# Byte offsets of the split weights in the gate and up tiles 2 and 3 of a two-layer decoder kernel

## Chip, cores and metric

The kernel runs on one core of one Trainium2 chip. The metric is the time of one execution on the device, in microseconds (us), lower is better. The engines are named as the profile names them: PE is the matmul engine (PEld are its weight loads), DVE the vector engine, ACT the scalar engine, POOL and SP the two others. SP issues the loads of the weights.

## What is computed

The reference is a decoder trunk of two layers on 256 tokens of width 1024, in float32. Each layer has a mixer (attention and Mamba heads in layer 0, a gated delta rule in layer 1), then a gated MLP with a short convolution, then a gated per-layer embedding. The change is in the MLP:

```python
def conv_ffn(h, w_gate, w_up, conv_w, conv_b, w_down):
    gte = causal_dwconv(h @ w_gate, conv_w) + conv_b.astype(h.dtype)
    return (jax.nn.silu(gte) * (h @ w_up)) @ w_down

for i in range(DEPTH):                      # DEPTH = 2
    ...
    h = rmsnorm(x, norm_ffn[i])
    x = x + conv_ffn(h, ffn_w_gate[i], ffn_w_up[i], ffn_conv_w[i], ffn_conv_b[i], ffn_w_down[i])
    x = x + per_layer_embedding(x, p[i], norm_ple[i], ple_w_proj[i], ple_w_gate[i])
```

`w_gate` and `w_up` are 1024 x 2816, `w_down` is 2816 x 1024.

## The kernel before

Activations lie transposed: 128 channels on the partitions, 256 tokens along a row. Every product of a weight matrix is made of blocks of 128 x 128 weights, and every block is used in three matmuls, because weights and activations are each split into a high part and a low part: high weights by high activations (line 187), high weights by low activations (line 188), low weights by high activations (line 189). Each of these matmuls streams 256 columns, and the engine loads its 128 x 128 weights for each of them anew. `mm3` (lines 179 to 189) writes these triples for the blocks of one accumulation.

`piece` (lines 140 to 167) brings weights in. For up to 1024 columns (`BLK`, eight blocks) it takes a buffer `raw`, lets SP issue the load from the weight stream, lets ACT write the high part `whi` (line 162), and lets DVE or POOL write the low part `wlo` (line 163). `whi` and `wlo` have four buffers each, and every buffer begins at a multiple of 256 bytes in its partition. The parameter `lead` shifts the weights within the buffer, in float32 columns of 4 bytes. The split operations are put into the order with a raised priority (`AHEAD`), so that they run ahead of the matmuls that need them.

The activations that the matmuls stream (`xx`, `yy`, `xp` and others) come from `moving` (lines 110 to 113): they begin 48 columns, so 192 bytes, behind a multiple of 256, and since each is 1024 bytes long, all of them lie 192 bytes behind such a multiple.

`ffn` (line 275 on) is the MLP of one layer. It runs over 22 tiles `f` of 128 channels. Each tile has 24 matmuls for the gate (into `pg`) and 24 for up (into `pu`), eight blocks of three each. DVE and ACT then make scaling, convolution, SiLU and product of the tile (lines 295 to 309) while PE is at the next tiles. Then follow eight tiles of the down projection (`pd`, 66 matmuls each), the projection of the embedding (`pp`, 48 matmuls in all), a norm (`nps`, `rep`) and its gate (`pgt`, 192 matmuls).

All tiles but one take their weights as two pieces of 1024 columns with `lead` 0: the gate's, then up's. Tile `f == KICK`, which is tile 2, is split by blocks: its first seven blocks come as two pieces of 896 columns with `lead` 48, so 192 bytes behind a multiple of 256, and the eighth block of both as one piece of 256 columns with `lead` 0.

```python
if f == KICK:
    for k0, nk, lead in ((0, 7, 48), (7, 1, 0)):
        ws = self.piece([(n, i, k0, nk, f * P, P) for _, n in both], lead=lead)
        for (ps, _), w in zip(both, ws):
            self.mm3(ps[:, :T], w, self.a[k0:k0 + nk], start=k0 == 0, stop=k0 == 7)
```

Of the kernel before, what the change touches and what calls it, by code (L numbers as in the profile page):

```python
# [8 lines left out]
F32R = mybir.dt.float32r  # L9
# [7 lines left out]
P = 128  # L17
BLK = 1024
# [3 lines left out]
KICK = 2  # L22
T = 256
D = 1024
KD = D // P
# [26 lines left out]
class Trunk:  # L52
# [84 lines left out]
        yield  # L137
        self.chain = was

    def piece(self, blocks, lo=None, lead=0):  # L140

        nc = self.nc
        groups, g, cols = [], [], 0
        for b in blocks:
            n = b[3] * b[5]
            if cols + n > BLK:
                groups.append((g, cols))
                g, cols = [], 0
            g.append(b)
            cols += n  # L150
        groups.append((g, cols))
        res = []
        for g, cols in groups:
            raw = self.rawp.tile([P, BLK], F32, tag="raw", name=self.uid("raw"))
            src = self.stream[self.off:self.off + P * cols].rearrange("(p c) -> p c", p=P)
            nc.sync.dma_start(raw[:, :cols], src)
            self.off += P * cols
            self.order.append(list(g))
            hi, lo_ = (self.splp.tile([P, BLK], F32R, tag=f"w{h}", name=self.uid(f"w{h}"), align_bytes=256)
                       [:, lead:lead + cols] for h in ("hi", "lo"))  # L160
            with self.tc.high_priority(offset=AHEAD):
                nc.scalar.activation(hi, raw[:, :cols], AF.Copy)  # L162
                self.lo_engine(lo).tensor_tensor(lo_, raw[:, :cols], hi.bitcast(F32), op=ALU.subtract)  # L163
            o = 0
            for (_, _, _, nk, _, w) in g:
                n = nk * w
                res.append((hi[:, o:o + n].rearrange("p (k f) -> p k f", f=w),
                            lo_[:, o:o + n].rearrange("p (k f) -> p k f", f=w)))
                o += n
        return res  # L170
# [105 lines left out]
    def ffn(self, i, nxt):  # L276
        nc, tc = self.nc, self.tc
        with self.psum(acc=7), tc.tile_pool(name=f"ffn{i}", bufs=3) as fp:
            ys = []
            yy = self.moving(fp, 2 * NF, "yy")  # L280
            for f in range(NF):
                pg, pu = self.acc("pg"), self.acc("pu")
                both = ((pg, "ffn_w_gate"), (pu, "ffn_w_up"))
                if f == KICK:

                    for k0, nk, lead in ((0, 7, 48), (7, 1, 0)):
                        ws = self.piece([(n, i, k0, nk, f * P, P) for _, n in both], lead=lead)
                        for (ps, _), w in zip(both, ws):
                            self.mm3(ps[:, :T], w, self.a[k0:k0 + nk], start=k0 == 0, stop=k0 == 7)
                else:  # L290
                    ws = self.piece([(n, i, 0, KD, f * P, P) for _, n in both])
                    for (ps, _), w in zip(both, ws):
                        self.mm3(ps[:, :T], w, self.a)
                g = fp.tile([P, T], F32, tag="g", name=self.uid("g"))
                nc.vector.tensor_tensor(g, pg[:, :T], self.R, op=ALU.mult)
                cw = lambda t: self.v(f"fcw{i}", f * 3 + t)
                h = fp.tile([P, T], F32, tag="h", name=self.uid("h"))
                nc.scalar.activation(h, g, AF.Identity, scale=cw(2), bias=self.v(f"fcb{i}", f))
                for s in (1, 2):
                    nc.vector.scalar_tensor_tensor(out=h[:, s:], in0=g[:, :T - s], scalar=cw(2 - s), in1=h[:, s:],  # L300
                                                   op0=ALU.mult, op1=ALU.add)
                sl = fp.tile([P, T], F32, tag="sl", name=self.uid("sl"))
                si = nc.scalar.activation(sl, h, AF.Silu)
                if i == 0 and f < len(self.zb[0]):
                    with tc.issue_after(si.ins):
                        nc.scalar.activation(self.zb[0][f], self.ident.unsqueeze(1).to_broadcast([P, 4, P]), AF.Copy)
                y = fp.tile([P, T], F32, tag="y", name=self.uid("y"))
                nc.vector.tensor_tensor(y, sl, pu[:, :T], op=ALU.mult)
                yh, yl = yy[2 * f:2 * f + 2]
                self.split(y, yh, yl)  # L310
                ys.append((yh, yl))
            self.norm_begin(f"ple{i}", fp)
            Rf = self.R
            for m in range(KD):
                pd = self.acc("pd")
                for k0, nk in ((0, 8), (8, 7), (15, 7)):
                    wd, = self.piece([("ffn_w_down", i, k0, nk, m * P, P)])
                    self.mm3(pd[:, :T], wd, ys[k0:k0 + nk], start=k0 == 0, stop=k0 == 15)
                d = fp.tile([P, T], F32, tag="pleg", name=self.uid("d"), bufs=4)
                nc.vector.tensor_tensor(d, pd[:, :T], Rf, op=ALU.mult)  # L320
                nc.vector.tensor_tensor(self.x[m], self.x[m], d, op=ALU.add)
                self.norm_tile(m)
            self.ple_proj(i, fp)
            self.norm_end()
            self.ple(i, nxt, fp)
# [831 lines left out]
```

## Time and profile before

| | us |
|---|---|
| median of three runs | 934.05 |
| lowest and highest of the three | 931.06, 934.14 |
| the profiled execution, its time | 932.68 |
| its span, first to last instruction | 930.9 |

| engine | busy, share of the span |
|---|---|
| PE | 98% |
| PE weight loads | 93% |
| DVE | 80% |
| ACT | 63% |
| POOL | 5% |

A busy PE says little of its own: a matmul's record is longer than the distance to the next one, since they are pipelined. How fast PE goes is read from the distance from one matmul's start to the next one's, called the pace here. A view by stretches counts every instruction that touches the stretch, so two or three of its matmuls began before it; the stretch divided by the count without these is the pace. The records of starts in the timeline are rounded to 10 ns, so a pace is taken over many matmuls.

### The profile page before, as it was taken

What the parts mean: (1) busy time and instruction counts of PE and PEld (TensorE: products, weight loads), DVE (VectorE), ACT (ScalarE), POOL (GpSimd) and SP (SyncE); (2) the same over time, 40 slices, a digit from 0 to 9 for tenths busy, and PEclk for the clock granted to TensorE, in tenths of its full rate; (3) what the DMA queues carried; (4) which work ended last, traced back from release to release, by engine and by line L of the source; (5) the groups of instructions that cost most, each with busy time, mean ns of one, the idle gap of its engine ahead of it and who ended that gap; (6) DMA issues with size and microseconds to landing.
All of it is one profiled execution on the core that took longest, in us unless ns stands there. A gap on an engine that the chain in (4) does not pass through costs nothing. (4 is left out here: it accounts for less than half of the span.)

```text
span 930.9 us, 19991 instructions
## 1 busy us (share of the span) xinstructions
PE 909.9 (98%) x7834; PEld 870.2 (93%) x7834; DVE 747.8 (80%) x1664; ACT 584.8 (63%) x1239; POOL 42.8 (5%) x53
## 2 busy tenths in 40 slices
PE   8999999999999999999989999999999999999998
PEld 6988778999999999989889999999999999999997
DVE  6977778978777766789989998999878877776665
ACT  6576565667555545667678778777656655554452
POOL 0000112100000001020000000000001000000100
PEclk9999999999999999999999999999999999999999
DMA  7543333456555556544413332432445655555571
GB/s 274 184 131 114 113 92 113 149 161 214 185 192 190 169 186 201 169 154 152 144 56 95 118 99 92 137 112 71 137 138 164 200 187 191 189 172 187 175 221 51
DMA packets 41278, 141.40 MB, mean 152 GB/s; under 512 B 4704, under 2 KB 6496, under 8 KB 41184
## 3 DMA queue, kind: packets, MB, share of 16 engines
q1 hardware_dynamic: 40896, 139.84, 46.9%
q8 instruction: 61, 1.00, 0.4%
q10 hardware_dynamic: 288, 0.29, 0.1%
q14 instruction: 33, 0.27, 0.1%
HBM read 139.06 MB, written 1.05 MB: 151 GB/s over the span
## 5 line engine op out<-in xcount | busy, mean ns | idle before, releaser
L162 ACT ACTIVATE whi<-raw 128x1024 fp32r<-128x1024 f32 (+3 forms) x268 | 277.7, 1037 | 189.2 <-PE pd L188 45.7
L163 DVE TENSOR_TENSOR wlo<-raw,whi 128x1024 fp32r<-128x1024 f32 (+3 forms) x268 | 320.2, 1195 | 86.5 <-ACT whi L162 83.6
L187 PE MATMUL pg<-xx,whi 128*128 128x256 f32 x352 | 99.0, 281 | 0.7 <-DVE x L707 0.3
L188 PE MATMUL pg<-xx,whi 128*128 128x256 f32 x352 | 99.0, 281 | 0.0
L187 PE MATMUL pu<-xx,whi 128*128 128x256 f32 x352 | 99.0, 281 | 0.0
L187 PE MATMUL pd<-yy,whi 128*128 128x256 f32 x352 | 98.9, 281 | 0.0
L188 PE MATMUL pd<-yy,whi 128*128 128x256 f32 x352 | 98.9, 281 | 0.0
L189 PE MATMUL pd<-yy,wlo 128*128 128x256 f32 x352 | 98.9, 281 | 0.0
L188 PE MATMUL pu<-xx,whi 128*128 128x256 f32 x352 | 98.8, 281 | 0.0
L189 PE MATMUL pu<-xx,wlo 128*128 128x256 f32 x352 | 98.8, 281 | 0.0
L189 PE MATMUL pg<-xx,wlo 128*128 128x256 f32 x352 | 98.8, 281 | 0.0
L187 PE MATMUL pgd<-xx,whi 128*128 128x256 f32 x256 | 75.7, 296 | 0.4 <-DVE z L993 0.4
L189 PE MATMUL pgd<-xx,wlo 128*128 128x256 f32 x256 | 74.7, 292 | 0.0
L188 PE MATMUL pgd<-xx,whi 128*128 128x256 f32 x256 | 74.5, 291 | 0.0
L187 PEld LDWEIGHTS pg<-xx,whi 128*128 128x128 f32 x352 | 67.4, 192 | 0.8 <-issue 0.8
L187 PEld LDWEIGHTS pd<-yy,whi 128*128 128x128 f32 x352 | 67.6, 192 | 0.0
L187 PEld LDWEIGHTS pu<-xx,whi 128*128 128x128 f32 x352 | 67.5, 192 | 0.0
L189 PEld LDWEIGHTS pg<-xx,wlo 128*128 128x128 f32 x352 | 66.1, 188 | 0.0
L189 PEld LDWEIGHTS pu<-xx,wlo 128*128 128x128 f32 x352 | 66.1, 188 | 0.0
L188 PEld LDWEIGHTS pg<-xx,whi 128*128 128x128 f32 x352 | 66.1, 188 | 0.0
L188 PEld LDWEIGHTS pu<-xx,whi 128*128 128x128 f32 x352 | 66.1, 188 | 0.0
L188 PEld LDWEIGHTS pd<-yy,whi 128*128 128x128 f32 x352 | 66.1, 188 | 0.0
(357 smaller groups left out, 2632.1 us busy)
## 6 DMA issues: line engine op xcount, KB each, us to landing
raw<-stream SPq DMA_DIRECT2D x228, 512.0 KB, 3.7
raw<-stream SPq DMA_DIRECT2D x36, 448.0 KB, 3.3
x<-xT SPq DMA_DIRECT2D x4, 256.0 KB, 4.9
out<-x SPq DMA_DIRECT2D x8, 128.0 KB, 1.8
cst<-cst SPq DMA_DIRECT2D x1, 645.0 KB, 5.9
raw<-pT SPq DMA_DIRECT2D x2, 256.0 KB, 2.6
raw<-stream SPq DMA_DIRECT2D x3, 128.0 KB, 2.1
pv<-pv ACTq DMA_DIRECT2D x1, 215.5 KB, 4.5
```

Of the source, the lines that this page charges most:

```text
L162: nc.scalar.activation(hi, raw[:, :cols], AF.Copy)
L163: self.lo_engine(lo).tensor_tensor(lo_, raw[:, :cols], hi.bitcast(F32), op=ALU.subtract)
L187: nc.tensor.matmul(out, wh, ah, start=start and k == 0, stop=False)
L188: nc.tensor.matmul(out, wh, al, start=False, stop=False)
L189: nc.tensor.matmul(out, wl, ah, start=False, stop=stop and k == n - 1)
```

## The change

The special case of tile 2 goes: it is loaded as two pieces of 1024 columns, as all others are. Buffers `whi` and `wlo` become 48 columns longer, and `lead` becomes a pair, the shift of a call's first piece and of its second. Tile 2 has (0, 16) and tile 3 has (32, 48), so the gate and up weights of these two tiles lie 0, 64, 128 and 192 bytes behind a multiple of 256. All others stay at 0.

```diff
-    def piece(self, blocks, lo=None, lead=0):
+    def piece(self, blocks, lo=None, lead=(0, 0)):
...
-        for g, cols in groups:
+        for n, (g, cols) in enumerate(groups):
...
-            hi, lo_ = (self.splp.tile([P, BLK], F32R, tag=f"w{h}", name=self.uid(f"w{h}"), align_bytes=256)
-                       [:, lead:lead + cols] for h in ("hi", "lo"))
+            at = lead[n % 2]
+            hi, lo_ = (self.splp.tile([P, BLK + 48], F32R, tag=f"w{h}", name=self.uid(f"w{h}"), align_bytes=256)
+                       [:, at:at + cols] for h in ("hi", "lo"))
...
-                if f == KICK:
-
-                    for k0, nk, lead in ((0, 7, 48), (7, 1, 0)):
-                        ws = self.piece([(n, i, k0, nk, f * P, P) for _, n in both], lead=lead)
-                        for (ps, _), w in zip(both, ws):
-                            self.mm3(ps[:, :T], w, self.a[k0:k0 + nk], start=k0 == 0, stop=k0 == 7)
-                else:
-                    ws = self.piece([(n, i, 0, KD, f * P, P) for _, n in both])
-                    for (ps, _), w in zip(both, ws):
-                        self.mm3(ps[:, :T], w, self.a)
+
+                ws = self.piece([(n, i, 0, KD, f * P, P) for _, n in both],
+                                lead={KICK: (0, 16), KICK + 1: (32, 48)}.get(f, (0, 0)))
+                for (ps, _), w in zip(both, ws):
+                    self.mm3(ps[:, :T], w, self.a)
```

On PE, at the end of tile 2 in layer 0, the order before is this. `pg_2719` and `pu_2720` are tile 2's accumulators, `whi_2729` and `wlo_2730` its up weights of 896 columns at 192 bytes, `whi_2777` and `wlo_2778` the piece with the eighth block of both at 0 bytes, and `pg_2800` is tile 3's gate.

```order
L189 MATMUL pu_2720<-xx_70,wlo_2730 128x256
L187 MATMUL pg_2719<-xx_70,whi_2777 128x256
L188 MATMUL pg_2719<-xx_70,whi_2777 128x256
L189 MATMUL pg_2719<-xx_70,wlo_2778 128x256
L187 MATMUL pu_2720<-xx_70,whi_2777 128x256
L188 MATMUL pu_2720<-xx_70,whi_2777 128x256
L189 MATMUL pu_2720<-xx_70,wlo_2778 128x256
L187 MATMUL pg_2800<-xx_70,whi_2804 128x256
```

In the changed kernel, where these lines are 188 to 190, the same place reads as follows; `pg_2794` is tile 3's gate, `whi_2729` and `wlo_2730` are tile 2's up weights at 64 bytes, `whi_2798` and `wlo_2799` tile 3's gate weights at 128 bytes.

```order
L188 MATMUL pu_2720<-xx_70,whi_2729 128x256
L189 MATMUL pu_2720<-xx_70,whi_2729 128x256
L190 MATMUL pu_2720<-xx_70,wlo_2730 128x256
L188 MATMUL pg_2794<-xx_70,whi_2798 128x256
L189 MATMUL pg_2794<-xx_70,whi_2798 128x256
L190 MATMUL pg_2794<-xx_70,wlo_2799 128x256
```

The gate's three matmuls of the eighth block moved from behind up's seventh block to the end of the gate's own; nothing else moved on PE, and there are as many matmuls as before.

On DVE, during tiles 1 and 2 of layer 0, the order before is this; `wlo` are the splits of weights, the other names belong to the tiles' elementwise work.

```order
L163 TENSOR_TENSOR wlo_2730<-raw_2727,whi_2729 128x896
L308 TENSOR_TENSOR y_2640<-sl_2637,pu_2570 128x256
L295 TENSOR_TENSOR g_2706<-pg_2644,Rrep_2555 128x256
L163 TENSOR_TENSOR wlo_2778<-raw_2775,whi_2777 128x256
L214 TENSOR_TENSOR yy_2568<-y_2640,yy_2568 128x256
L300 SCALAR_TENSOR_TENSOR h_2708<-g_2706,pv,h_2708 128x255
L300 SCALAR_TENSOR_TENSOR h_2708<-g_2706,pv,h_2708 128x254
L308 TENSOR_TENSOR y_2715<-sl_2712,pu_2645 128x256
L163 TENSOR_TENSOR wlo_2805<-raw_2802,whi_2804 128x1024
```

In the changed kernel the same place on DVE reads so.

```order
L164 TENSOR_TENSOR wlo_2730<-raw_2727,whi_2729 128x1024
L304 TENSOR_TENSOR y_2640<-sl_2637,pu_2570 128x256
L291 TENSOR_TENSOR g_2706<-pg_2644,Rrep_2555 128x256
L164 TENSOR_TENSOR wlo_2799<-raw_2796,whi_2798 128x1024
L215 TENSOR_TENSOR yy_2568<-y_2640,yy_2568 128x256
L296 SCALAR_TENSOR_TENSOR h_2708<-g_2706,pv,h_2708 128x255
L296 SCALAR_TENSOR_TENSOR h_2708<-g_2706,pv,h_2708 128x254
L164 TENSOR_TENSOR wlo_2805<-raw_2802,whi_2804 128x1024
L304 TENSOR_TENSOR y_2715<-sl_2712,pu_2645 128x256
```

The small split of 256 columns is gone, and the split of tile 3's gate weights stands in its place. ACT and SP lose one instruction per layer in the same way.

## Rows read from the trace of the kernel before

**Rows 1.** The page: span, and each engine's busy time, share and instructions.

```profile
span 930.9 us, 19991 instructions
...
PE 909.9 (98%) x7834; PEld 870.2 (93%) x7834; DVE 747.8 (80%) x1664; ACT 584.8 (63%) x1239; POOL 42.8 (5%) x53
```

**Rows 2.** Stretches: length; busy (count) of PE, PEld, DVE, ACT, POOL; clock; DMA.

```profile
172.00:190.00 18.00, 18.00 (x162) 18.00 (x161) 16.54 (x24) 13.13 (x23) 4.25 (x5) 1.00 0.56 177
198.17:203.61 5.44, 5.44 (x51) 5.44 (x49) 4.27 (x9) 4.42 (x8) 0.00 (x0) 1.00 0.65 197
203.61:208.64 5.03, 5.03 (x44) 5.03 (x43) 3.32 (x5) 3.26 (x5) 0.00 (x0) 1.00 0.42 118
209.35:319.60 110.25, 110.25 (x939) 110.25 (x938) 87.47 (x139) 65.69 (x104) 0.00 (x0) 1.00 0.59 192
385.80:388.20 2.40, 2.40 (x23) 2.40 (x23) 2.19 (x9) 0.27 (x1) 0.00 (x0) 1.00 0.48 179
389.50:408.20 18.70, 18.70 (x161) 18.70 (x161) 16.69 (x31) 12.90 (x26) 3.63 (x5) 1.00 0.46 147
715.58:721.02 5.44, 5.44 (x51) 5.44 (x49) 4.37 (x9) 4.04 (x7) 0.00 (x0) 1.00 0.68 207
721.02:726.06 5.04, 5.04 (x45) 5.04 (x43) 3.22 (x5) 2.73 (x4) 0.00 (x0) 1.00 0.48 148
726.76:834.20 107.44, 107.44 (x915) 107.44 (x914) 85.67 (x137) 62.21 (x97) 0.00 (x0) 1.00 0.59 189
834.20:902.00 67.80, 67.80 (x578) 67.80 (x577) 44.53 (x55) 35.45 (x53) 5.89 (x6) 1.00 0.61 194
```

**Rows 3.** Tile pg, 198.2 to 203.4 us (tile 1): durations min/median/max, ns.

```profile
L187 PEld LDWEIGHTS pg<-xx,whi x8: 187/188/188, 198.1 to 200.4; 128*128 128x128 f32 x8
L187 PE MATMUL pg<-xx,whi x8: 276/276/276, 198.2 to 200.5; 128*128 128x256 f32 x8
```

**Rows 4.** Tile pg, 204 to 206 us (tile 2, weights at 192 bytes).

```profile
L187 PEld LDWEIGHTS pg<-xx,whi x6: 192/192/192, 203.8 to 205.6; 128*128 128x128 f32 x6
L187 PE MATMUL pg<-xx,whi x6: 283/283/283, 204.0 to 205.8; 128*128 128x256 f32 x6
```

**Rows 5.** Tile pg, 209.4 to 319.5 us (tiles 3 to 21).

```profile
L187 PEld LDWEIGHTS pg<-xx,whi x152: 192/192/192, 209.2 to 313.5; 128*128 128x128 f32 x152
L187 PE MATMUL pg<-xx,whi x152: 281/281/281, 209.3 to 313.6; 128*128 128x256 f32 x152
L188 PEld LDWEIGHTS pg<-xx,whi x152: 187/188/188, 209.4 to 313.6; 128*128 128x128 f32 x152
```

**Rows 6.** Timeline of PE, layer 0: start, duration, into and out of tile 2.

```profile
203.49 0.28 PE L189 MATMUL pu<-xx,wlo 128*128 128x256 f32 x1
203.61 0.28 PE L187 MATMUL pg<-xx,whi 128*128 128x256 f32 x1
203.73 0.28 PE L188 MATMUL pg<-xx,whi 128*128 128x256 f32 x1
...
208.53 0.28 PE L189 MATMUL pu<-xx,wlo 128*128 128x256 f32 x1
208.64 0.28 PE L187 MATMUL pg<-xx,whi 128*128 128x256 f32 x1
208.76 0.28 PE L188 MATMUL pg<-xx,whi 128*128 128x256 f32 x1
```

**Rows 7.** Lines by shape, DVE's splits: count | busy us, mean ns | idle before, releaser.

```profile
L163 DVE TENSOR_TENSOR wlo<-raw,whi 128x1024 fp32r<-128x1024 f32 x228 | 279.3, 1226 | 57.2 <-ACT whi L162 54.3
...
L163 DVE TENSOR_TENSOR wlo<-raw,whi 128x896 fp32r<-128x896 f32 x36 | 39.4, 1093 | 29.3 <-ACT whi L162 29.3
```

**Rows 8.** Timeline of DVE in layer 0: start, length, idle time before.

```profile
199.29 1.09 DVE L163 TENSOR_TENSOR wlo<-raw,whi 128x896 fp32r<-128x896 f32 x1
...
202.01 0.43 DVE L163 TENSOR_TENSOR wlo<-raw,whi 128x256 fp32r<-128x256 f32 x1
...
205.83 1.23 DVE L163 TENSOR_TENSOR wlo<-raw,whi 128x1024 fp32r<-128x1024 f32 x1 [1.05 <-ACT whi L162]
```

## The prediction

> **What bounds the kernel now.** I read the page first: PE is busy for 909.9 of 930.9 us [rows 1]. Since a busy PE can still go at different speeds, the second view is the one by stretches, and what to see there is that inside the MLPs PE fills every stretch to the last digit (5.44 of 5.44 us, 110.25 of 110.25) at a granted clock of 1.00, the 2.4 GHz level [rows 2]. So no wait ends there, neither for weights nor for DVE or ACT, and the only thing that can move the time of an MLP is PE's pace. I get it by dividing a stretch by its matmuls, less the two or three that began earlier:
>
> - tile 1 of layer 0: 5.44 us / 48 = 113.3 ns; layer 1 the same, 5.44 / 48 [rows 2];
> - tile 2, the blocks with weights at 192 bytes: 5.03 / 42 = 119.8 ns, layer 1 5.04 / 42 = 120.0 [rows 2];
> - tile 3 and on: 110.25 / 936 = 117.8 ns; in layer 1 107.44 / 912 = 117.8, and 67.80 / 575 = 117.9 through the down projection and `pp` [rows 2].
>
> All of these are the same instructions of the same shape; only the offset of the weights differs in the second, and not even that between the first and the third. The durations say the same: 276 ns a matmul and 187 to 188 a weight load in tile 1 [rows 3], 283 and 192 in tile 2 [rows 4], 281 ns and one load of three at 192, the others at 187 to 188, from tile 3 on [rows 5]. The timeline dates the changes: the step from 113 to 120 ns comes with the first matmuls whose weights lie at 192 bytes (203.49, 203.61, 203.73), and the first matmuls with weights at 0 again (208.64, 208.76) leave the 120 at once, but for 117.8 and not for 113.3 [rows 6].
>
> So offset 0 has **two paces, and the stream remembers which**. Outside the MLP's tiles this shows too: 18.00 us / 159 = 113.2 ns in layer 0's output projection, and in one and the same loop of `pgt` 2.40 / 21 = 114 ns before the norm's replication comes between and 18.70 / 159 = 117.6 ns behind it [rows 2]. A stream keeps its pace until something interrupts it. In the MLP of before the interruption is tile 2, and it leaves the rest of the MLP, the down projection and `pp`, at the slower pace.
>
> **The change part by part.** Per layer, from tile 2's first matmul to the end of `pp`:
>
> Before: tile 2 is 42 x 119.8 + 6 x 117.8 = 5.03 + 0.71 = 5.74 us, tile 3 is 48 x 117.8 = 5.65 us, together 11.39 us. Behind them come tiles 4 to 21 (18 x 48 = 864 matmuls), the down projection (8 x 66 = 528) and `pp` (48): 1440 x 117.8 = 169.6 us.
>
> After, tile 2's gate at 0 bytes just goes on from tile 1: 24 x 113.3 = 2.72 us. Up of tile 2 at 64 and gate of tile 3 at 128 bytes are offsets that no row of before has. I bound them by the two paces next to them, 113.3 and 119.8 ns, so 2.72 to 2.88 us each. The activations lie at 192 bytes; the row with the higher price is the one where the weights lie at the same place as the activations, and 64 and 128 differ from 192 as 0 does, so I take the lower end for both. They could not be much better than that, since 113.3 is the fastest pace anywhere in the rows. Up of tile 3 at 192 bytes repeats what tile 2 does now: 24 x 119.8 = 2.88 us. Sum 3 x 2.72 + 2.88 = 11.04 us, 0.35 less than 11.39 in each layer; at the upper ends 11.36, so 0.03 less. For both layers that is 0.7, or 0.1.
>
> The term that decides is the pace of the 1440 matmuls behind. What I forecast is the exit: tile 3's up brings the stream to 120 ns by the same offset as now, and the next weights are at 0, as now. Before, this exit ended in 117.8 in layer 0 and in layer 1 alike [rows 2], and the step was immediate [rows 6]. The exit falls between the same two kinds of matmul, line 189 of up and line 187 of the next gate, and in both kernels nothing waits there. So the 1440 cost 169.6 us as before, a difference of 0. If that is wrong and the exit leads to 113.3, they cost 163.2 us.
>
> The rest lies beside PE. In each layer one load, one split on ACT and one on DVE go away; DVE does 2 x 1226 instead of 2 x 1093 + 430 ns for tile 2, 0.16 us less [rows 7, 8]. I cost this at nothing, since PE's stretch has no gap. The cover is the lead of the splits: tile 3's first split ends at 205.83 + 1.23 = 207.06 us [rows 8], and tile 3 begins at 209.35, 2.3 us later. With the small piece gone it is earlier in DVE's order. Were the lead gone, each piece of 1024 columns would cost PE up to a split of 1226 ns; nothing speaks for that. The longer buffers move addresses by multiples of 256 bytes, and the rows' paces don't depend on those: each block's weights begin 512 bytes further than the last one's, and the pace stays the same over 936 matmuls [rows 2].
>
> Sum: 932.68 - 0.7 = 932.0 us for the profiled execution, whose span of 930.9 has 1.8 us around it. It lies 1.4 below the median of the three runs, 934.05, within their spread of 931.06 to 934.14. On the median's scale I forecast 934.05 - 0.7 = **933.3 us**.
>
> **A page that speaks against this.** The trace shows 113.3 and 119.8 ns for matmuls that differ in the byte offset of their weights [rows 2]. The Trainium skill, page "SBUF — State Buffer", section "SBUF: two separate sides", says of the engines' ports that "PE, ACT, and DVE's dedicated pair never wait on anyone". By that rule an offset would cost nothing, and tile 2's pace would need another cause. The trace so far disagrees: a load takes 192 instead of 188 ns just where the offset is 192 bytes [rows 3, 4].
>
> **The rivals.**
>
> - *The walk releases the fast pace.* Four steps of 64 bytes instead of one of 192 could bring the stream back to offset 0 at 113.3 ns, since that pace exists there. For it: `pgt` changes its pace at an interruption, so an exit need not always be the same. Against it: the last step, 192 to 0, is the one that twice ended in 117.8. Price: 1440 x (117.8 - 113.3) = 6.5 us per layer, 13.0 for both, and 0.7 from the tiles: 934.05 - 13.7 = 920.4 us. Chance 0.22. If only one layer does it, about 927: 0.04.
> - *The offset does nothing, and the split of tile 2 into seven blocks and one did it.* Then the change takes away the cause, and all from tile 2 on stays at 113.3: (11.39 + 169.6) - 1536 x 113.3 = 7.0 us per layer, so 934.05 - 14.0 = 920.0 us. Against it: the pace changes at the first weights at 192, not at the piece's end, and the down projection, two of whose three pieces per tile have 896 columns (32 of the 36 in the kernel [rows 7]), keeps its pace. Chance 0.06; here the change doesn't do what it says, and the shifts are without effect.
> - *The slow pace of 192 bytes is kept,* the end on the other side. A stream that remembers a pace at offset 0 might remember this one too when it arrives by 128 and not by 0 bytes. Place: from tile 4 to `pp`; price 1440 x (119.8 - 117.8) = 2.9 us per layer, 5.8 less the 0.7: 939.1 us. It decides the sign as soon as one layer keeps even a quarter of it, 0.7 us. Against it: the exit of before left 120 within one matmul, and no stretch at offset 0 in the rows is above 117.9. Chance 0.08.
>
> **How the numbers follow.** My forecast, the exit as before, has 0.60. Its own range is the spread of the three runs, about 3 us, and the bounds of 0.1 to 0.7: 931 to 936. About 0.5% (4.7 us) is what a measurement of this kernel can tell from no change. Faster by more than that are the first rival in both its forms and the second: 0.22 + 0.04 + 0.06 = 0.32. Slower by more is the third: 0.08, and the rest, 0.60, is within 0.5%. The range has to take in the fast cases, since they hold 0.32, and may leave out the slow one: 918.5 to 937.
>
> **What would show it.** In the stretches of the changed kernel: tile 2's gate at 113.3 ns, its up and tile 3's gate between 113.3 and 120, tile 3's up at 120 with loads of 192 ns, and tile 4 to `pp` at 117.8 with one load of three at 192. If tile 4 begins at 113.3 with all loads at 188, the first rival is right; if tile 3's up shows 113.3 as well, the second; at 120 beyond tile 4, the third. What would make all of this wrong is a gap in PE at tiles 2 to 4, or another pace already in tile 1 of either layer.

## The result and the profile after

| | before | after |
|---|---|---|
| median of four runs each, us | 933.14 | 920.63 |
| lowest and highest, us | 931.06, 934.14 | 920.39, 923.28 |
| the profiled execution, us | 932.68 | 923.28 |

The ratio is 0.9871, with a 95% interval of 0.9851 to 0.9892: the changed kernel is 1.3% faster. The forecast was 933.3 us; 920.63 is close to the time of its first rival, 920.4.

The page of the changed kernel, the lines that answer to [rows 1]:

```profile
span 921.5 us, 19977 instructions
...
PE 900.1 (98%) x7834; PEld 860.1 (93%) x7834; DVE 747.3 (81%) x1662; ACT 584.8 (63%) x1237; POOL 42.9 (5%) x53
```

As many matmuls as before, and 9.4 us less of span. The view by stretches, as in [rows 2], of tile 1, of tile 2's gate (0 bytes) and up (64), of tile 3's gate (128) and up (192), of tiles 4 to 21 and of the down projection, all in layer 0, then tile 3's up and tiles 4 to 21 in layer 1:

```profile
198.80:204.24 5.44, 5.44 (x51) 5.44 (x49) 3.61 (x6) 5.27 (x8) 0.00 (x0) 1.00 0.56 181
204.24:206.96 2.72, 2.72 (x26) 2.72 (x25) 2.69 (x5) 1.98 (x4) 0.00 (x0) 1.00 0.41 107
206.96:209.80 2.84, 2.84 (x27) 2.84 (x25) 2.17 (x5) 1.95 (x4) 0.00 (x0) 1.00 0.83 277
209.80:212.63 2.83, 2.83 (x27) 2.83 (x25) 2.70 (x5) 2.07 (x4) 0.00 (x0) 1.00 0.57 153
212.63:215.51 2.88, 2.88 (x26) 2.88 (x25) 2.29 (x4) 1.81 (x3) 0.00 (x0) 1.00 0.74 232
215.51:313.44 97.93, 97.93 (x867) 97.93 (x865) 79.44 (x128) 59.69 (x93) 0.00 (x0) 1.00 0.61 191
313.44:373.28 59.84, 59.84 (x531) 59.84 (x529) 40.63 (x50) 30.51 (x42) 5.95 (x6) 1.00 0.63 199
...
726.38:729.27 2.89, 2.89 (x26) 2.89 (x25) 2.29 (x4) 1.82 (x3) 0.00 (x0) 1.00 0.62 186
729.27:827.20 97.93, 97.93 (x867) 97.93 (x865) 79.44 (x128) 58.10 (x90) 0.00 (x0) 1.00 0.63 192
```

A half tile has 24 matmuls, so 2.72 us is a pace of 113.3 ns, 2.83 is 117.9, 2.88 is 120.0. Tile 2's gate stays at 113.3; up at 64 bytes goes at 118.2, the gate at 128 at 117.9, up at 192 at 120.2. And then the rest is at 113.3: 97.93 / 864, 59.84 / 528, in both layers, where before it was 117.8 [rows 2]. PE is again busy to the last digit of every stretch.

The timeline of PE at the exit from 192 bytes (start, duration), to be held against the second half of [rows 6]:

```profile
215.39 0.28 PE L190 MATMUL pu<-xx,wlo 128*128 128x256 f32 x1
215.51 0.28 PE L188 MATMUL pg<-xx,whi 128*128 128x256 f32 x1
215.63 0.28 PE L189 MATMUL pg<-xx,whi 128*128 128x256 f32 x1
215.75 0.28 PE L190 MATMUL pg<-xx,wlo 128*128 128x256 f32 x1
215.86 0.28 PE L188 MATMUL pg<-xx,whi 128*128 128x256 f32 x1
215.97 0.28 PE L189 MATMUL pg<-xx,whi 128*128 128x256 f32 x1
```

Three matmuls after the first gate weights at 0 bytes the distance falls from 0.12 to 0.11 us and stays there. The view by tile tells that the two stays at 192 bytes are not the same. In [rows 4] every load took 192 ns and every matmul's record 283. Here, for tile 3's up (min/median/max, ns), and below it for the gates of tiles 4 to 21:

```profile
L188 PEld LDWEIGHTS pu<-xx,whi x7: 188/188/190, 212.9 to 215.0; 128*128 128x128 f32 x7
L188 PE MATMUL pu<-xx,whi x7: 280/283/287, 213.0 to 215.1; 128*128 128x256 f32 x7
...
L188 PE MATMUL pg<-xx,whi x143: 276/276/276, 215.9 to 310.4; 128*128 128x256 f32 x143
L189 PEld LDWEIGHTS pg<-xx,whi x143: 187/188/188, 215.9 to 310.4; 128*128 128x128 f32 x143
```

Same offset, nearly the same mean pace, but loads of 188 to 190 ns and matmuls that differ among themselves.

Where the time went, by the starts in the two timelines: from tile 2's first matmul to `pgt`'s first, 181.8 us before and 175.3 after, in each layer, so 13.0 us gained; layer 0's `pgt` (the embedding's gate) 0.7 more, since it came out of its interruption at the faster pace this time. Given back in the profiled execution: 0.6 us before layer 0's MLP, and 3.5 between `pgt` and layer 1's MLP (300.6 us before, 304.1 after). The latter is seen in the granted clock at the start of layer 1's mixer; first the kernel before, then the same place of the changed one:

```profile
409.50:416.00 6.50, 5.41 (x46) 5.00 (x47) 5.20 (x16) 3.73 (x8) 0.73 (x1) 1.00 0.45 164
```

```profile
403.10:409.60 6.50, 5.36 (x35) 4.77 (x35) 4.52 (x11) 3.48 (x8) 0.77 (x2) 0.74 0.55 168
```

There the clock stood at its 1.2 GHz level for a part of the stretch, which it didn't before (0.74 against 1.00). The profiled execution is the slowest of the four, 923.28 against 920.39 to 920.74 us; its mean granted clock was 0.992 and that of the others 0.995 to 0.996, so by these clocks little of this loss is in the gain of 12.5 us at the medians.

### The profile page after: what moved, and what is told of

Read it like the earlier page. It is cut to its first block, busy times and chain, and to the rows that moved or that the text cites. A ratio compares the mean times of both kernels' runs of the same rounds, so it can differ in the third digit from the quotient of the medians.

```text
span 921.5 us, 19977 instructions
## 1 busy us (share of the span) xinstructions
PE 900.1 (98%) x7834; PEld 860.1 (93%) x7834; DVE 747.3 (81%) x1662; ACT 584.8 (63%) x1237; POOL 42.9 (5%) x53
## 5 line engine op out<-in xcount | busy, mean ns | idle before, releaser
L163 ACT ACTIVATE whi<-raw 128x1024 fp32r<-128x1024 f32 (+2 forms) x266 | 277.7, 1044 | 176.8 <-PE pd L189 38.6
L164 DVE TENSOR_TENSOR wlo<-raw,whi 128x1024 fp32r<-128x1024 f32 (+2 forms) x266 | 319.8, 1202 | 81.8 <-ACT whi L163 79.7
L188 PE MATMUL pg<-xx,whi 128*128 128x256 f32 x352 | 97.4, 277 | 0.6 <-DVE x L703 0.3
L188 PE MATMUL pu<-xx,whi 128*128 128x256 f32 x352 | 97.5, 277 | 0.0
L189 PE MATMUL pg<-xx,whi 128*128 128x256 f32 x352 | 97.4, 277 | 0.0
L189 PE MATMUL pu<-xx,whi 128*128 128x256 f32 x352 | 97.4, 277 | 0.0
L188 PE MATMUL pd<-yy,whi 128*128 128x256 f32 x352 | 97.2, 276 | 0.0
L189 PE MATMUL pd<-yy,whi 128*128 128x256 f32 x352 | 97.2, 276 | 0.0
```

Source lines behind the costliest of these rows:

```text
L188: nc.tensor.matmul(out, wh, ah, start=start and k == 0, stop=False)
L189: nc.tensor.matmul(out, wh, al, start=False, stop=False)
```

## The experiments

Theory A: a stream of these matmuls keeps its pace at offset 0 until something moves it, and what moves it is the way by which the weights' offset changes. The others are named where they come. All diffs are against the changed kernel but one. In what follows "fast" is 113.3 ns at 0 bytes, "slow" 117.8.

**No shift at all.**

```diff
-                                lead={KICK: (0, 16), KICK + 1: (32, 48)}.get(f, (0, 0)))
+                                lead={}.get(f, (0, 0)))
```

> All weights of all tiles at 0 bytes, nothing else changed against the changed kernel. Theory A (a stream keeps its pace until something shifts it): tiles 0 and 1 run at 113.3 ns, so tiles 2 and 3 and the 1440 matmuls behind do too; tiles 2 and 3 then take 96 x 113.3 = 10.88 instead of 11.28 us in each layer, 920.6 - 0.8 = 919.8 us. Theory B (the walk is what makes the fast pace, a stream left alone falls back to 117.8 somewhere in the MLP): up to 1440 x 4.5 = 6.5 us per layer more, 926 to 933 us.

Measured 927.01 us at the median, ratio to the kernel before 0.9892 (0.9851 to 0.9934), but the five executions are 919.21, 920.76, 927.01, 927.16 and 928.03: two levels. Stretches from tile 1 on in layer 0 and in layer 1 of the profiled one (927.16 us):

```profile
198.31:315.00 116.69, 116.69 (x1032) 116.69 (x1031) 94.66 (x151) 74.12 (x115) 0.00 (x0) 1.00 0.60 192
708.00:830.00 122.00, 122.00 (x1038) 122.00 (x1037) 95.26 (x152) 71.32 (x110) 0.00 (x0) 1.00 0.59 182
```

116.69 / 1029.5 = 113.3 ns and 122.00 / 1035.5 = 117.8. Nothing falls back: layer 0 begins fast and stays, layer 1 begins slow and stays. So a fast stream needs no walk, theory B falls, and a layer can come in slow by itself. Theory A's time, 919.8, was met in two executions of five, since its premise, that every layer begins at 113.3, holds only in some. That layers are slow in the two other executions near 927 is read from their times alone.

**192 bytes at once, back at 0 at a tile's start.**

```diff
-                                lead={KICK: (0, 16), KICK + 1: (32, 48)}.get(f, (0, 0)))
+                                lead={KICK + 1: (0, 48)}.get(f, (0, 0)))
```

> Only tile 3's up lies at 192 bytes, all else at 0: the walk's last step without the two steps before it, and with weights back at 0 at a tile's start. Theory A (the way to 192 decides): 120.0 ns there with all weight loads at 192 ns, then 117.8 ns from tile 4 on in both layers, some 933 us. Theory C (the place decides where the weights return to 0: at a tile's start, and no longer between a tile's seventh and eighth block): 113.3 ns from tile 4 on, some 920 us.

933.08 us, ratio 0.9992 (0.9981 to 1.0004). Tile 3's gate, its up, tile 4's gate, and a long stretch behind, in layer 0:

```profile
208.50:211.22 2.72, 2.72 (x26) 2.72 (x25) 2.69 (x5) 2.00 (x3) 0.00 (x0) 1.00 0.56 191
211.22:214.10 2.88, 2.88 (x26) 2.88 (x25) 2.28 (x5) 1.86 (x3) 0.00 (x0) 1.00 0.70 236
214.10:216.93 2.83, 2.83 (x27) 2.83 (x25) 2.34 (x4) 1.95 (x4) 0.00 (x0) 1.00 0.61 190
...
215.00:315.00 100.00, 100.00 (x851) 100.00 (x850) 78.20 (x124) 58.89 (x93) 0.00 (x0) 1.00 0.56 187
```

The same last step and the same exit at a tile's start as in the changed kernel, and it ends slow. What differs is only how the stream got to 192. Theory C, the place, falls; the way decides.

**The split of before without its shift** (against the kernel before).

```diff
-                    for k0, nk, lead in ((0, 7, 48), (7, 1, 0)):
+                    for k0, nk, lead in ((0, 7, 0), (7, 1, 0)):
```

> The kernel before with its split of tile 2 into seven blocks and one, but all at 0 bytes. Theory A (the shift did it): 113.3 ns through tile 2 and to the end of the embedding's projection, about 920 us. Theory D (the split did it): 120 and then 117.8 ns as before, 933 us.

926.47 and 919.06 us. In the execution of 926.47, layer 0 behind tile 2, then layer 1:

```profile
210.00:315.00 105.00, 105.00 (x928) 105.00 (x928) 86.44 (x138) 64.84 (x102) 0.00 (x0) 1.00 0.60 199
708.00:713.00 5.00, 5.00 (x45) 5.00 (x44) 3.56 (x8) 4.09 (x7) 0.00 (x0) 1.00 0.44 124
720.00:830.00 110.00, 110.00 (x936) 110.00 (x935) 86.86 (x138) 64.09 (x99) 0.00 (x0) 1.00 0.59 190
```

Layer 0 goes through the split and stays fast (105.00 / 926 = 113.4). Layer 1 is slow, and was so in its tile 1 already, ahead of the split (5.00 us for 42.5 matmuls). It behaves like the kernel without any shift; theory D falls. Its buffers have the old length, those of the two runs before it the new one: with the new length 192 bytes at once ended slow as in the kernel before, and with the old one layer 0 stays fast, so the length of the buffers isn't what decides.

**First slow, then the walk.**

```diff
-                                lead={KICK: (0, 16), KICK + 1: (32, 48)}.get(f, (0, 0)))
+                                lead={KICK: (0, 48), KICK + 2: (0, 16), KICK + 3: (32, 48)}.get(f, (0, 0)))
```

> Tile 2's up at 192 bytes at once, tile 3 at 0, then the walk 0, 64, 128, 192 in tiles 4 and 5. It asks whether the walk mends a slow stream or only doesn't harm a fast one. If 192 at once leaves 117.8 ns in tile 3 and the walk mends: 113.3 from tile 6 on, about 921 us. If the walk only keeps a pace: 117.8 from tile 6 on, about 933 us. If place decides (theory C): 113.3 already in tile 3 and from tile 6 on, about 921 us.

934.41 us, ratio 0.9998 (0.9987 to 1.0010). Layer 1, from tile 2's up (192 at once): tile 3's up at 0, tile 4's up at 64, tile 5's gate at 128 and up at 192, tile 6's gate at 0:

```profile
726.07:728.95 2.88, 2.88 (x27) 2.88 (x26) 2.20 (x5) 1.86 (x3) 0.00 (x0) 1.00 0.63 188
...
731.77:734.60 2.83, 2.83 (x27) 2.83 (x25) 2.25 (x4) 1.80 (x3) 0.00 (x0) 1.00 0.54 187
...
737.43:740.28 2.85, 2.85 (x27) 2.85 (x25) 2.27 (x4) 1.79 (x3) 0.00 (x0) 1.00 0.55 185
740.28:743.10 2.82, 2.82 (x26) 2.82 (x25) 2.15 (x4) 1.43 (x3) 0.00 (x0) 1.00 0.49 186
743.10:745.97 2.87, 2.87 (x26) 2.87 (x25) 2.29 (x4) 1.80 (x3) 0.00 (x0) 1.00 0.50 183
745.97:748.80 2.83, 2.83 (x27) 2.83 (x25) 2.13 (x4) 1.43 (x3) 0.00 (x0) 1.00 0.49 185
```

The walk passes on what came in: slow in, slow out. In layer 0 of the same execution the stream was slow by itself, in tile 1 already (197.50 to 203.16 us for its 48 matmuls, 117.9 ns), and it left the walk at 117.8 as well. On its way it has other paces than in the changed kernel, 118.7 instead of 118.2 at 64 and 119.6 instead of 120.2 at 192. So the changed kernel gains because its layers begin fast and its walk doesn't make them slow, while before's one step did.

**The changed kernel once more**, since a layer can begin slow. No diff.

> The changed kernel once more, to see whether its time has two levels. Without any shift there were two: 919 to 921 and 927 to 928 us, the latter with one layer at 117.8 ns from tile 1 on. Theory A (the walk passes on the pace that a layer came with): of ten executions or so, several near 927 us, whenever a layer begins slow. Theory E (the changed kernel's layers always begin fast, or the walk mends some of the slow ones): all between 919 and 924 us.

922.64, 920.93, 921.55 and 920.50 us, ratio 0.9869 (0.9853 to 0.9886). With the first four, eight executions, and none near 927, as theory E says. By the run before, the walk doesn't mend slow layers, so these should all have begun fast; two of them were profiled, and both layers began fast there. Why the kernels without a shift began slow in some of theirs, and this one in none, isn't settled. All seven executions without a shift ran on one chip and these four on another (the chip of the first four isn't known), so the chip may have a part in it: that the changed kernel always begins fast isn't shown.

**Many steps in one kernel,** in units of 4 bytes.

```diff
-                                lead={KICK: (0, 16), KICK + 1: (32, 48)}.get(f, (0, 0)))
+                                lead={2: (16, 0), 4: (32, 0), 6: (0, 16), 7: (32, 0), 9: (48, 0),
+                                      11: (16, 0), 13: (32, 0), 15: (48, 32), 16: (16, 0), 18: (0, 16), 19: (32, 48)}.get(f, (0, 0)))
```

> Many steps in one kernel, each followed by half a tile or more at 0 bytes where the pace is read: tile 2's gate at 64; tile 4's gate at 128; tile 6's up at 64 and tile 7's gate at 128; tile 9's gate at 192; then from the slow stream tile 11's gate at 64, tile 13's at 128, tile 15 and 16 the walk back 192, 128, 64, and tiles 18 and 19 the walk of the changed kernel. Theory A (192 at once is what makes a stream slow, and nothing among these mends it): 113.3 ns at 0 bytes up to tile 8, 117.8 from tile 10 on. Theory F (64 or 128 bytes alone are enough to turn a stream, in either direction): other paces already in tile 3, 5 or 8, or 113.3 again in tile 12, 14 or 17. The time says little: by A some 927 us with both layers slow from tile 10.

924.95 us, one execution. From layer 0: tile 4's gate (128) and up; tile 7's gate (128, behind 64) and up; tile 13's gate (128, from slow) and up:

```profile
215.32:218.04 2.72, 2.72 (x27) 2.72 (x25) 2.37 (x4) 1.89 (x3) 0.00 (x0) 1.00 0.48 166
218.04:220.76 2.72, 2.72 (x27) 2.72 (x25) 2.04 (x5) 1.86 (x3) 0.00 (x0) 1.00 0.64 223
...
231.76:234.59 2.83, 2.83 (x27) 2.83 (x25) 2.28 (x4) 1.43 (x3) 0.00 (x0) 1.00 0.57 185
234.59:237.41 2.82, 2.82 (x26) 2.82 (x25) 2.23 (x4) 1.80 (x3) 0.00 (x0) 1.00 0.53 187
...
265.76:268.58 2.82, 2.82 (x26) 2.82 (x25) 2.18 (x4) 1.42 (x3) 0.00 (x0) 1.00 0.61 190
268.58:271.31 2.73, 2.73 (x27) 2.73 (x26) 2.14 (x4) 1.80 (x3) 0.00 (x0) 1.00 0.61 197
```

128 bytes cost a fast stream nothing if it comes from 0, and 117.9 ns if it comes by 64; in the second case the exit ends slow. And 128 coming from a slow stream at 0 turns it fast. Theory A, as it is put for this run, falls in both halves: 64 and then 128 bytes make a stream slow without any step to 192, and 128 mends. Theory F is right for 128; 64 alone turned nothing.

**Finer offsets.**

```diff
-                                lead={KICK: (0, 16), KICK + 1: (32, 48)}.get(f, (0, 0)))
+                                lead={2: (8, 0), 4: (24, 0), 6: (40, 0), 8: (48, 0),
+                                      10: (8, 0), 12: (24, 0), 14: (40, 0), 16: (8, 16), 17: (24, 32), 18: (40, 48)}.get(f, (0, 0)))
```

> As the run before, with offsets between the multiples of 64: tile 2's gate at 32 bytes, tile 4's at 96, tile 6's at 160, tile 8's at 192; from the slow stream tile 10's gate at 32, tile 12's at 96, tile 14's at 160, and in tiles 16 to 18 a walk in steps of 32 from 32 to 192. Theory A: 113.3 ns at 0 bytes up to tile 7, 117.8 from tile 9 on. Theory G (a finer step drags a slow stream into the fast pace): 113.3 in tile 11, 13, 15 or from tile 19 on.

931.71 us, one execution. Tile 2's gate at 32 bytes from fast; tile 8's up behind 192; tile 10's gate at 32 from slow, and its up:

```profile
204.59:207.48 2.89, 2.89 (x27) 2.89 (x25) 2.85 (x6) 2.07 (x4) 0.00 (x0) 1.00 0.40 109
...
240.52:243.35 2.83, 2.83 (x27) 2.83 (x25) 2.28 (x4) 1.76 (x3) 0.00 (x0) 1.00 0.57 191
...
249.00:251.82 2.82, 2.82 (x27) 2.82 (x25) 2.18 (x4) 1.42 (x3) 0.00 (x0) 1.00 0.51 184
251.82:254.54 2.72, 2.72 (x27) 2.72 (x25) 2.12 (x4) 1.81 (x3) 0.00 (x0) 1.00 0.64 199
```

32 bytes mend a slow stream too and leave a fast one fast; while they last, they cost 120 ns from fast and 117 from slow. The next two offsets, 96 and 160, then met a fast stream again, so for them only that direction is known. The walk in steps of 32 from 32 to 192 ended slow. Theory G is right for a single step of 32 and wrong for the walk.

Both kernels showed the same paces in both layers, to 0.2 ns. Put together, with what a fast and a slow stream pass through and end in:

| offsets, then 0 | from fast | from slow |
|---|---|---|
| 64 | 118.2, ends fast | 118.6, ends slow |
| 128 | 113.3, ends fast | 117.7, ends fast |
| 192 | 119.9, ends slow | 119.9, ends slow |
| 64, 128 | 118.1, 118.0, ends slow | |
| 64, 128, 192 | 118.1, 117.9, 120.3, ends fast | 118.7, 117.7, 119.6, ends slow |
| 192, 128, 64 | 120.0, 113.5, 118.2, ends fast | |
| 32 | 120.1, ends fast | 117.2, ends fast |
| 96; 160 | 119.6; 116.5, end fast | |

**One half tile at 128 bytes.**

```diff
-                                lead={KICK: (0, 16), KICK + 1: (32, 48)}.get(f, (0, 0)))
+                                lead={KICK: (32, 0)}.get(f, (0, 0)))
```

> One half tile per layer at 128 bytes (tile 2's gate), all else at 0. The many-step run showed a fast stream pass 128 bytes at 113.3 ns and a slow one leave it fast. Theory H (128 bytes mends, and costs nothing): tile 3 and all behind at 113.3 ns in both layers in every execution, no second level near 927 us; against the changed kernel 96 x 113.3 = 10.88 instead of 11.28 us per layer, so 0.8 us less, 920 us. Theory A alone (a stream keeps what it has): two levels, 919 and 927 us.

920.90 us (918.42 to 922.05), ratio to the kernel before 0.9859 (0.9841 to 0.9877); the changed kernel's is 0.9871 (0.9851 to 0.9892), so the two aren't told apart by time. Tile 1 on in layer 0, and in layer 1 from within tile 2's gate on, 113.3 ns both:

```profile
198.00:315.00 117.00, 117.00 (x1035) 117.00 (x1034) 94.89 (x151) 74.07 (x115) 0.00 (x0) 1.00 0.61 192
718.00:830.00 112.00, 112.00 (x991) 112.00 (x990) 90.38 (x144) 66.22 (x103) 0.00 (x0) 1.00 0.63 193
```

The 0.4 us per layer that the walk costs are gone from the stretches. Both layers began fast in this execution, so it doesn't show the mending; the last run does.

**Every piece by turns at 0 and 128, and all at 128.**

```diff
-            at = lead[n % 2]
+            at = 32 * (len(self.order) % 2)
```

(for the second run, `at = 32`; in both, `lead` is not used.)

> Every piece of weights in the whole kernel lies by turns at 0 and at 128 bytes. Theory H: a slow stream is mended wherever it arises, within two pieces; in the kernel of before some 370 matmuls of layer 1's mixer, 320 of the embedding's gates and in some runs 160 of the output projection are at 117.8 ns, so up to 2 to 3 us less than the run before this one, 917 to 919 us. Theory I (changing to and fro is itself what makes a stream slow somewhere): paces of 117.8 ns in the MLP, over 921 us.

920.30 us (919.62 to 920.92), ratio 0.9855 (0.9838 to 0.9871). The MLPs are fast from tile 2 on. In layer 0 tile 1 still went at 117.7 ns (197.90 to 203.55 us for its 48 matmuls): a stream that had become slow by itself was fast two pieces later, as theory H says. The expected 2 to 3 us below the run with one half tile did not come: the two medians are 0.6 us apart, and their intervals overlap. The runs don't show why.

> All weights of the whole kernel at 128 bytes. If 128 bytes is an offset with one pace alone, 113.3 ns everywhere and 916 to 919 us; if it has two as offset 0 has, 113.3 in layers that begin fast and 117.6 in others, 919 to 933 us.

935.48 us, one execution, and the stretches of both layers from tile 1 on:

```profile
200.00:315.00 115.00, 115.00 (x979) 115.00 (x978) 90.16 (x144) 69.91 (x110) 0.00 (x0) 1.00 0.58 186
720.00:830.00 110.00, 110.00 (x937) 110.00 (x936) 85.96 (x138) 64.14 (x100) 0.00 (x0) 1.00 0.61 185
```

117.8 ns in both: 128 bytes for good is no cure. Both layers were slow in tile 1 already, so the run shows that lying at 128 doesn't mend a slow stream, and the run with many steps that a fast one goes at 113.3 there. What turned a slow stream in the runs was a step from 0 to 128 (or to 32) and back, not the place.

**First slow, then one half tile at 128.**

```diff
-                                lead={KICK: (0, 16), KICK + 1: (32, 48)}.get(f, (0, 0)))
+                                lead={KICK: (0, 48), KICK + 2: (32, 0)}.get(f, (0, 0)))
```

> Both layers are made slow on purpose, by tile 2's up at 192 bytes at once, and then tile 4's gate alone lies at 128 bytes. It is the run with the walk behind a slow stream, with the walk's two tiles replaced by one half tile. Theory H (128 bytes mends a slow stream): tile 3 at 117.8 ns, tile 4's gate at 117.6, its up and all behind at 113.3, about 921 us. Theory A alone (a slow stream stays slow): 117.8 ns to the end of the MLP, about 933 us.

923.48 us (920.45 to 923.51), ratio 0.9882 (0.9852 to 0.9911). Tile 3's up at 0, tile 4's gate at 128 and up at 0, and a long stretch behind, in layer 0:

```profile
212.55:215.38 2.83, 2.83 (x27) 2.83 (x25) 2.24 (x4) 1.80 (x3) 0.00 (x0) 1.00 0.63 221
215.38:218.20 2.82, 2.82 (x26) 2.82 (x25) 2.18 (x4) 1.94 (x4) 0.00 (x0) 1.00 0.59 187
218.20:220.92 2.72, 2.72 (x26) 2.72 (x25) 2.13 (x4) 1.80 (x3) 0.00 (x0) 1.00 0.68 199
...
217.00:315.00 98.00, 98.00 (x867) 98.00 (x866) 79.24 (x127) 59.46 (x93) 0.00 (x0) 1.00 0.62 193
```

A stream made slow by the same step as in the run with the walk behind it, which stayed slow there at 934.41 us, is fast here after 24 matmuls at 128 bytes. Layer 1 shows the same paces.

## Why the prediction was right in its range and wrong in its likeliest case

- **What bounds the kernel:** right. PE fills the MLPs before and after, and the gain there is pace: of 6.5 us per layer 6.4 are the 1440 matmuls at 113.3 instead of 117.8 ns.
- **Tile 2's gate at 113.3:** right, 2.72 us.
- **64 and 128 bytes at the lower bound of 113.3:** wrong end. Up at 64 measured 2.84 us and the gate at 128 2.83, so tiles 2 and 3 took 11.28 us and not 11.04, within the bounds given (11.04 to 11.36). The reason, that an offset costs only where it equals the activations', is refuted: 64 cost 118.2 and 128 either 113.3 or 117.9, by the way there.
- **192 bytes at 119.8:** right in size, 2.88 us, wrong in kind. I took the stay at 192 for one that forgets what was before it. It doesn't: loads of 188 to 190 instead of 192 ns showed another state of the stream.
- **The exit:** here the forecast failed. "The next weights are at 0, as now", and so 117.8 behind, rested on two exits that had both come by the same way, straight from 0. The run with 192 at once shows that way ending slow, the changed kernel the walk ending fast. The 1440 matmuls cost 163.2 and not 169.6 us per layer, the number that the text gave for this case.
- **The range** held because it was widened for the rivals; the forecast's own range, 931 to 936, missed.
- **The first rival** had the place and the price: 13.7 us, where the stretches gained 13.0 and the medians 12.5. That its 920.4 lies so near to 920.63 is partly luck, since the median before was 933.14 with the fourth run and not 934.05. Of its mechanism, that the walk releases the fast pace, half is shown: a stream that comes in fast leaves the walk fast, a slow one leaves it slow. It had 0.22 because I held its last step against it. The text itself said that a stream remembers its pace at offset 0; carried to offset 192, that was a reason to put the rival and the forecast nearer to each other.
- **The second rival,** that the split and not the offset did it, falls with the split at 0 bytes. 192 bytes alone, with no other edit against the kernel without a shift, change the pace from 113.3 to 120.0 ns. So what I drew from the Trainium skill (page "SBUF — State Buffer", section "SBUF: two separate sides"), that an offset costs nothing since PE never waits on anyone, does not hold for this case, and the measurement decides. My own sign against it was misread: loads of 192 ns do not come "just where the offset is 192 bytes". One load of three took 192 at 0 bytes too [rows 5], and tile 3's up of the changed kernel had none at 192 bytes.
- **The third rival** didn't occur: no long stretch behind an exit to 0 bytes was above 117.8 ns in any run.
- **The work beside PE** cost nothing, as said.

Shown: both paces persist at 0 bytes, the way decides, 128 bytes from 0 mends. Not shown: what in the memory or the engine makes the two states; no run here looks inside. The loads of 192 ns are no sure sign of the slow one either: with all weights at 128 bytes the stream went at 117.8 ns, and its loads took 187 to 188. And why some layers begin slow, without a shift, stays open.

## What to carry to other kernels

Where a matmul stream is bound by its own pace, read the pace over long stretches and compare equal instructions: two paces for the same instructions mean that the stream has states, and a place where it changes can be worth more than an instruction removed. Here the state was set by history, so two equal observations by one path say little of another path; give a change of the path a high chance of another end. If a long stream can start in either state, a short shift that ends fast from both (here 24 matmuls at 128 bytes) is safer than one that only passes on what comes.

## What the runs showed that was not expected

A stream of equal matmuls at a granted clock of 1.00 went at 113.3 or at 117.8 ns for as long as 1440 matmuls, and all weights lying 128 bytes further on were at 117.8 in both MLPs, so neither 0 nor 128 bytes is fast by itself. The kernel without a shift has two levels of time some 7 us apart for this, 919 to 921 and 927 to 928 us. And part of a gain on PE can be lost behind it. In the profiled execution PE waited 2.01 us for DVE ahead of layer 1's mixer, where it waited 1.48 before, and the 1.2 GHz level followed:

```profile
404.24 0.28 PE L188 MATMUL pab<-xx,whi 128*32 128x256 f32 x1 [2.01 <-DVE pleg L353]
```

The traces of all thirteen profiled executions, before, after and in the experiments, agree on the wait. In six of them layer 0's `pgt` came out of its interruption at 117.8 ns; it then took 23.1 us, and PE waited 1.5. In the seven others it went on at 113.3 (113.6 in the run by turns), took 22.4 to 22.5, and PE waited 2.0, so 0.5 of the 0.7 us gained in `pgt` went into the wait. The clock is less regular. Behind a wait of 1.5 us it stayed at 1.00 in all six. Behind 2.0 it was 0.74 in five of the seven; in the run with many steps and in the last one it stayed at 1.00, as here in the last one:

```profile
403.07:409.57 6.50, 5.05 (x43) 4.66 (x43) 5.23 (x15) 3.49 (x8) 0.77 (x2) 1.00 0.56 171
```

So the drop came only behind the longer wait, but not each time. No run changed the wait by itself.
